# Sparse attention heads of a hybrid encoder block: negated logits, scaling by ScalarE, operands of two heads in one step, and some query copies by GpSimd's queue

## The chip, the cores and the metric

The kernel runs on one core of one Trainium2 chip. The metric is the device time of one execution in microseconds, as a median over runs; 439.57 us before the change. A profile of one execution gives the rows that this document quotes. In them PE is TensorE (its matmuls), PEld its weight loads, DVE is VectorE, ACT is ScalarE, POOL is GpSimd and SP is SyncE, which issues most DMAs. A name with a q (SPq, POOLq) is the engine's instruction queue. L389 is line 389 of the kernel's source.

## The reference

One pre-norm layer on x of 512 x 1024 in float32, with two token mixers that share one input projection. Cut to what matters:

```python
h = rmsnorm(x, norm_g)
(q_lat, c_kv, k_rope, z_a, q_b, k_b, v_b, z_b, q_idx, k_idx, w_idx, gate_a, gate_b) = split(h @ w_in)
# A: latent attention, 8 heads of 64 + 32 rotary, chunk-causal (chunks of 64)
y_a = mla_attention(...) * silu(z_a)
# B: sparse attention, 8 heads of 64; an indexer of 8 heads of 32 scores the keys
s     = einsum('qhd,kd->qhk', q_idx, k_idx) * 32 ** -0.5
score = einsum('qhk,qh->qk', relu(s), w_idx * 8 ** -0.5)      # inadmissible keys: -inf
idx   = top_k(score, 128)                                     # 128 keys for each query
logits = q_b . k_b[idx] * 64 ** -0.5 + rel_bias[t5_bucket(idx - pos)]
y_b   = softmax(logits) @ v_b[idx] * silu(z_b)
merged = sigmoid(gate_a) * (y_a @ w_o_a) + sigmoid(gate_b) * (y_b @ w_o_b)
out = rmsnorm(x + merged @ w_out, final_g)
```

## The kernel before

Every float32 product is made of products of rounded parts: an operand x is split into a high part (ScalarE rounds it) and a low part x - high (VectorE or GpSimd subtracts), and a product is high*high + high*low + low*high, three matmuls (`mm3`, recorded at L389).

The sparse heads do not gather keys. For each of the four tiles of 128 queries, the indexer's scores (`scores`) become a mask (`topk`: 16 rounds of the eight largest, for three tiles), which is 0 for chosen keys and -1e30 for the others. `dsa_base` loads the relative bias of a head and adds the mask (`s_p<-s_bias,mask`), so that a head starts from a tile `p` with bias plus mask. `dsa_head` then makes the logits of one tile on TensorE, and its `soft` adds them to `p` and takes the row maximum in one VectorE instruction (L1248), negates the maximum (L336, called from `soft`), applies the exponential on ScalarE with the row sum as a side result (L300), takes the reciprocal (L1142) and scales the row (`normalise`, by VectorE at L347 or GpSimd at L350). `attend` transposes the probabilities on TensorE (L406), splits them again and multiplies them with the values.

`dsa_jobs(j)` prepares the operands of heads 2j and 2j+1, which come out of one projection as rows 0 to 63 and 64 to 127 of one PSUM bank. A query operand is one tile with the high part in the head's own 64 rows and the low part in the other 64; a key operand is a tile with the high part in both halves and one with the low part in both halves. So two matmuls of 128 rows make the four products. `take_q` does this head by head with ScalarE and VectorE, each of which writes across to the other half; `take_k` makes the head's own half with these engines and the other half by a copy (`s_op<-s_op`, 128 KB, by SP's queue).

For the indexer, `take_qi` makes the query operand of each of eight heads out of three pieces of 32 rows, by 24 copies (`s_qs<-s_th`, 64 KB). The pieces whose number is below `QPOOL` go by GpSimd's queue, the others by SP's; `QPOOL` is 0.

The order of all work on every engine is fixed when the program is built. `Flow` is a planner: every piece of work is a generator that yields steps with one or more engines that may do them and an expected duration each, and waits for buffers (`Get`) or conditions (`Until`). At each turn the planner places the step that can start first, with a priority of 0.01 us per unit to break near ties; where a step may go to several engines, it takes the one that would end first, with a handicap or bonus for GpSimd (`pbias`) and for ScalarE (`ABIAS`, 0). On the chip each engine goes through its instructions in that order and waits for what they need. A DMA issued by SP is charged 0.05 us of SP, 0.65 us of the issuing hardware when both ends are tiles, 0.65 us more, its bytes at 360 GB/s, and 2.2 us till it has landed (1.0 us where it comes from or goes to HBM). A DMA by GpSimd is charged 1.03 us of that engine.

Weights come through four raw buffers (`fetcher`), are split into at most eight slots (`splitter`), and are used in the order of a list, `QUEUE` (`multiplier`): gates (ga, gb), silu paths (za, zb), head projections (ma, sb), values (va, vb). The four `sb` entries stand among gates and silu paths. The last products of the branches (`branch_out`, `s_ys,s_w`) come after all of them, first branch A's eight, then branch B's, and then those with `w_out`. TensorE fills with this list whenever no head's step can start sooner. Two lanes run the sparse heads, even and odd ones.

Of the kernel before, what the change touches and what calls it, by code (L numbers as in the profile page):

```python
# [13 lines left out]
AF = mybir.ActivationFunctionType  # L14
# [4 lines left out]
P = 128  # L19
# [60 lines left out]
class Step:  # L80


    moves = 0.0
    pair = False
    pbias = None
# [45 lines left out]
class Flow:  # L131
# [46 lines left out]
    def run(self, stop=None):  # L178
        while self.threads:
            if stop and stop():  # L180
                return
            moved = False
            for t in sorted(self.threads, key=lambda t: t.prio):
                if isinstance(t.req, Get):
                    b = t.req.pool.give(t.req)
                    if b is not None:
                        self.advance(t, b)
                        moved = True
                elif isinstance(t.req, Until) and t.req.cond():
                    self.advance(t, None)  # L190
                    moved = True
            if moved:
                continue
            best = None
            for t in self.threads:
                if isinstance(t.req, Step):
                    for i, (eng, dur, emit) in enumerate(t.req.options):
                        s = self.start(t.req, eng)
                        key = (s + BIAS * t.prio, t.prio)
                        if len(t.req.options) > 1:  # L200
                            fin = s + dur + {"POOL": self.pbias if t.req.pbias is None else t.req.pbias, "ACT": ABIAS}.get(eng, 0.0)
# [32 lines left out]

RAW_LAG = {"DVE": 0.125, "POOL": 0.1, "ACT": 0.1}
BIAS = 0.01
ABIAS = 0.0
TC_ARGS = {}


# [1 line left out]
def tile_block(ctx: ExitStack, tc: tile.TileContext, a: dict, out: bass.AP, bias_dram: bass.AP):  # L242
# [61 lines left out]
    def act(dst, src, func=AF.Copy, scale=None, bias=None, accum=None):  # L304
        step = Step([act_opt(dst, src, func, scale, bias, accum)], bufs(dst, accum), bufs(src, scale, bias))
        step.count = 2 if accum is not None else 1
        return step
# [886 lines left out]

    def dsa_jobs(j):
        def take_q(ps):
            yield Until(lambda: ("a", NH - 1, 0) in operands)
            for b in range(2):
                own, oth = slice(64 * b, 64 * b + 64), slice(64 - 64 * b, 128 - 64 * b)
                q = yield Get(QHI)  # L1200
                yield act(q[own, :], ps[own, :], AF.Copy, scale=HD ** -0.5)
                yield stt(q[oth, :], ps[own, :], HD ** -0.5, q[own, :].f, ALU.mult, ALU.subtract)
                operands["b", 2 * j + b, 0] = q
            put(ps)

        def take_k(ps):
            for b in range(2):
                own, oth = slice(64 * b, 64 * b + 64), slice(64 - 64 * b, 128 - 64 * b)
                kh = yield slot("op")
                kl = yield slot("op")  # L1210
# [12 lines left out]
    def dsa_base(h):  # L1223

        yield is_done("bias", *(("mask", i) for i in range(1, NT)))
        yield Until(lambda: h < 2 or ("b", h - 2) in done)
        bias = yield slot("bias")
        yield dma(bias.all.f, bass.AP(bias_dram.tensor, h * NREL + 1, [[1, P], [1, S]]))
        slots, probs = yield from prob_tiles("p", 6)
        for i in range(NT):  # L1230
            n = P * (i + 1)
            yield tt(probs[i], backward(bias.all.f[:, :n]), mask[i].all, ALU.add, BOTH)
        put(bias)
        bases[h] = (slots, probs)

    def dsa_head(h):
# [7 lines left out]
        def soft(i, ps):  # L1244
            n = P * (i + 1)
            mx = yield Get(SMALL)
            p = probs[i]
            step = Step([("DVE", 0.1 + 0.00104 * n, lambda: nc.vector.tensor_tensor_reduce(  # L1248
                p.ap, ps.tile[:, :n], p.ap, op0=ALU.add, op1=ALU.max, scale=1.0, scalar=FILL,
                accum_out=mx.tile[:, 0:1]))], [mx, p.buf], [ps])  # L1250
            step.count = 2
            yield step
            put(ps)
            yield ts(mx[:, 1:2], mx[:, 0:1], -1.0, None, ALU.mult)
            yield act(p, p, AF.Exp, bias=mx[:, 1:2], scale=1.0, accum=mx[:, 2:3])
            yield from normalise(p, mx)
            put(mx)
            ready.add(i)

# [366 lines left out]
PSQ = 0.0  # L1626
PSET = 0.0
NORM = ('DVE', 'POOL')
NWARM = 7
XAT = 1  # L1630
QPOOL = 0
PHCAP = 4
WCAP = 8
TCAP = 5
# [89 lines left out]
```

## Time and profile before

| | before |
|---|---|
| median of 3 runs | 439.57 us (439.42 to 441.98) |
| the profiled execution | 439.49 us |
| its span, first to last instruction | 437.7 us |
| TensorE busy | 426.2 us, 2219 matmuls |
| TensorE weight loads busy | 364.7 us |
| VectorE busy | 345.1 us, 810 instructions |
| ScalarE busy | 244.6 us, 546 instructions |
| GpSimd busy | 125.3 us, 150 instructions |
| mean granted TensorE clock | 0.998 |

The execution lasts 1.8 us longer than its span. Matmuls are pipelined, so that a busy TensorE need not be at its peak; DMA-issuing instructions are not counted as busy. In a row of a group, the number after the bar is the group's busy time in us, then the mean duration of one in ns, and after the next bar the idle time of the engine just before them and what ended it.

### The profile page before, as it was taken

To read this page: it belongs to the slowest core of one execution; us is meant where nothing else is said; L and a number is where in the kernel's file an instruction comes from. 1 tells how busy PE (TensorE), PEld (TensorE's weight loads), DVE (VectorE), ACT (ScalarE), POOL (GpSimd) and SP (SyncE) were. 2 spreads that over 40 slices of the span, in tenths; PEclk is the share of its full clock that TensorE was granted. 3 is DMA by queue.
4 is the path that set the end of the run, shared out by engine and by line. 5 is a ranking of instruction groups with operands and counts; after the bars stand their busy time and mean duration, and the time that the engine had idled before them with its cause. 6 is when DMAs were issued, how large, how long until landed. Compare 5 with 4: busy or idle time off the path is not lost.

```text
span 437.7 us, 6862 instructions
## 1 busy us (share of the span) xinstructions
PE 426.2 (97%) x2219; PEld 364.7 (83%) x2219; DVE 345.1 (79%) x810; ACT 244.6 (56%) x546; POOL 125.3 (29%) x150
## 2 busy tenths in 40 slices
PE   8999999999999999999999999999999999999994
PEld 5899878888887888878899888998888888888883
DVE  5599589999999999794343977835776686999995
ACT  6976877557472757364333654734565553345633
POOL 2256966544555634000003120050000011001452
PEclk9999999999999999999999999999999999999999
DMA  8973441725337361414541216234116445538405
GB/s 260 393 251 92 111 146 55 204 82 138 98 84 209 79 185 33 120 43 144 145 148 45 73 73 144 82 112 133 60 50 216 168 152 185 179 111 288 145 1 192
DMA packets 26500, 59.45 MB, mean 136 GB/s; under 512 B 4072, under 2 KB 4600, under 8 KB 26464
## 3 DMA queue, kind: packets, MB, share of 16 engines
q1 hardware_dynamic: 25744, 58.05, 43.2%
q0 software_dynamic: 576, 0.83, 0.7%
q8 instruction: 17, 0.28, 0.3%
q14 instruction: 19, 0.16, 0.1%
q10 hardware_dynamic: 144, 0.13, 0.1%
HBM read 48.39 MB, written 2.12 MB: 115 GB/s over the span
## 4 chain that ended last, share of the span: by engine, by line
PE 73%; DVE 13%; DMA 4%; ACT 4%; issue 2%; POOL 1%; SPq 1%; POOLq 0%; DVEq 0%; ACTq 0%
PE ps L389 67%; PE ps L406 4%; DVE mask L787 3%; DVE sm L786 3%; DMA s_op<-s_op 2%; DVE sm L1163 1%; DMA raw<-w_kvl 1%; DMA s_op<-kpel 1%; ACT junk L300 1%; PE ps L764 1%; SPq L416 1%; DVE s_ph L317 1%; PE ps L1182 1%; DVE qhi L328 1%; DVE s_op L328 1%
## 5 line engine op out<-in xcount | busy, mean ns | idle before, releaser
L389 PE MATMUL ps<-s_h,s_w 128*128 128x512 f32 x768 | 189.4, 394 | 0.0
L389 PEld LDWEIGHTS ps<-s_h,s_w 128*128 128x128 f32 x768 | 140.9, 188 | 26.7 <-issue 0.2
L319 POOL TENSOR_TENSOR s_w<-raw,s_w 128x512 fp32r<-128x512 f32 (+2 forms) x38 | 45.1, 1197 | 99.0 <-DMA raw<-w_out 64.3
L291 ACT CAST s_w<-raw 128x512 fp32r<-128x512 f32 (+3 forms) x114 | 64.3, 591 | 4.2 <-PE ps L389 2.1
L317 DVE TENSOR_TENSOR s_w<-raw,s_w 128x512 fp32r<-128x512 f32 (+2 forms) x76 | 49.2, 670 | 12.2 <-ACT s_w L291 11.8
L319 POOL TENSOR_TENSOR s_p<-s_bias,mask 128x128 f32<-128x128 f32 (+3 forms) x19 | 14.4, 785 | 102.9 <-DMA s_bias<-bias_scratch 90.3
L389 PE MATMUL ps<-s_ys,s_w 128*128 128x512 f32 x192 | 43.7, 389 | 0.0
L389 PEld LDWEIGHTS ps<-s_ys,s_w 128*128 128x128 f32 x192 | 36.0, 188 | 7.5
L389 PE MATMUL ps<-s_wo,s_mg 128*128 128x512 f32 (+1 forms) x156 | 33.0, 373 | 0.0
L389 PE MATMUL ps<-s_w,s_xg 128*128 128x328 f32 (+1 forms) x192 | 32.4, 324 | 0.0
L389 PEld LDWEIGHTS ps<-s_w,s_xg 128*128 128x128 f32 x192 | 31.5, 188 | 0.8 <-DVE s_w L317 0.2
L389 PEld LDWEIGHTS ps<-s_wo,s_mg 128*128 128x128 f32 x156 | 27.6, 188 | 5.2
L787 DVE MATCH_REPLACE8 mask<-sm,mask 128x256 f32<-128x256 f32 (+2 forms) x48 | 25.9, 541 | 0.0
L786 DVE MAX8 sm<-mask 128x8 f32<-128x256 f32 (+2 forms) x48 | 25.6, 549 | 0.3
L300 ACT ACTIVATE s_p<-ps,sm 128x128 f32<-128x128 f32 (+3 forms) x32 | 16.8, 527 | 15.2 <-DVE sm L1163 13.4
L389 PE MATMUL ps<-s_w,s_h 128*128 128x256 f32 x192 | 23.8, 284 | 0.0
L389 PEld LDWEIGHTS ps<-s_w,s_h 128*128 128x128 f32 x192 | 23.4, 192 | 0.2
L300 ACT ACTIVATE s_p<-s_p,sm 128x128 f32<-128x128 f32 (+3 forms) x32 | 17.8, 558 | 9.9 <-DVE sm L336 9.8
L406 PE MATMUL ps<-ident,s_p 128*128 128x128 f32 x160 | 22.9, 273 | 0.0
L300 ACT ACTIVATE s_sig<-ps 128x512 f32<-128x512 f32 x16 | 9.6, 597 | 22.7 <-PE ps L389 22.5
L350 POOL TENSOR_SCALAR s_p<-s_p,sm 128x128 f32<-128x128 f32 (+3 forms) x31 | 16.1, 527 | 19.0 <-DVE sm L1142 18.8
L389 PE MATMUL ps<-s_lat,s_w 128*128 128x512 f32 x78 | 21.4, 398 | 0.0
(164 smaller groups left out, 723.5 us busy)
## 6 DMA issues: line engine op xcount, KB each, us to landing
raw<-w_out SPq DMA_DIRECT2D x18, 512.0 KB, 4.2
raw<-w_ga SPq DMA_DIRECT2D x8, 512.0 KB, 4.3
raw<-w_gb SPq DMA_DIRECT2D x8, 512.0 KB, 3.6
raw<-w_o SPq DMA_DIRECT2D x16, 256.0 KB, 3.8
s_op<-s_op SPq DMA_DIRECT2D x28, 128.0 KB, 2.3
s_x<-xT SPq DMA_DIRECT2D x8, 256.0 KB, 5.4
s_xn<-x SPq DMA_DIRECT2D x8, 256.0 KB, 5.4
raw<-w_za SPq DMA_DIRECT2D x4, 512.0 KB, 4.2
```

Of the source, the lines that this page charges most:

```text
L291: nc.scalar.copy(dst.ap, src.ap)
L300: nc.scalar.activation(dst.ap, src.ap, func, **kw)
L317: opts.append(("DVE", 0.07 + 0.00104 * x.n, lambda: nc.vector.tensor_tensor(dst.ap, x.ap, y.ap, op=op)))
L319: opts.append(("POOL", 0.15 + 0.0021 * x.n, lambda: nc.gpsimd.tensor_tensor(dst.ap, x.ap, y.ap, op=op)))
L328: lambda: nc.vector.scalar_tensor_tensor(dst.ap, x.ap, sc(s), y.ap, op0=op0, op1=op1))],
L350: lambda: nc.gpsimd.tensor_scalar(dst.ap, x.ap, s.ap, 1.0, ALU.mult, ALU.mult)))
L389: nc.tensor.matmul(ps.ap, l.ap, r.ap, start=start and i == 0, stop=stop and i == len(pairs) - 1, skip_group_check=more)
L406: nc.tensor.transpose(d.ap, s.ap, ident.tile)
L416: return Step([("SP", n / 360000.0, lambda: nc.sync.dma_start(d, s))], bufs(dst), bufs(src))
L764: yield pe(0.005 + n / 2400, [ps.all], [qs[h].all, ks[0].all], lambda: nc.tensor.matmul(ps.tile[:, :n], qs[h].tile[:96, TOK[i]], ks[0].til ...
L786: yield Step([("DVE", t, lambda: nc.vector.max(m8.tile, work.tile))], [m8], [work])
L787: yield Step([("DVE", t, lambda: nc.vector.match_replace(work.tile, m8.tile, work.tile, MARK))], [work], [m8])
```

## The change

Four things.

In `soft` of the sparse heads the VectorE instruction computes -(logits + p) and takes the row minimum, which is the negated maximum. The separate negation goes, and the exponential is taken with scale -1.

The scaling of the sparse heads' rows may go to VectorE or ScalarE instead of VectorE or GpSimd, and the planner counts ScalarE as ending 0.5 us earlier than it would (`NORM_BIAS`). The heads of branch A keep VectorE or GpSimd.

`take_q` and `take_k` split both heads' rows at once, with one ScalarE and one VectorE instruction of 128 rows, and bring the halves to their places by copies on SP's queue: three for the queries of a pair, six for the keys. A copy that overwrites rows waits until the copies that read them are done.

`QPOOL` becomes 1: 8 of the indexer's 24 copies are issued by GpSimd. Besides, the planner counts the load of a head's bias as landing 1.5 us later (`late`).

```diff
@@ Flow.run
-                            fin = s + dur + {"POOL": ..., "ACT": ABIAS}.get(eng, 0.0)
+                            fin = s + dur + {"POOL": ..., "ACT": t.req.abias}.get(eng, 0.0)
...
-                end = self.dma + (2.2 if step.ins and step.outs else 1.0)
+                end = self.dma + (2.2 if step.ins and step.outs else 1.0) + step.late
@@ normalise
-    def normalise(p, mx):
+    def normalise(p, mx, engs=None):
         yield Step([("DVE", 0.07, lambda: nc.vector.reciprocal(mx.tile[:, 3:4], mx.tile[:, 2:3]))], [mx], [mx])
-        yield scale_by(p, p, mx[:, 3:4], NORM)
+        step = scale_by(p, p, mx[:, 3:4], engs or NORM)
+        step.abias = NORM_BIAS if engs else 0.0
+        yield step
@@ dsa_jobs
         def take_q(ps):
             yield Until(lambda: ("a", NH - 1, 0) in operands)
-            for b in range(2):
-                own, oth = slice(64 * b, 64 * b + 64), slice(64 - 64 * b, 128 - 64 * b)
-                q = yield Get(QHI)
-                yield act(q[own, :], ps[own, :], AF.Copy, scale=HD ** -0.5)
-                yield stt(q[oth, :], ps[own, :], HD ** -0.5, q[own, :].f, ALU.mult, ALU.subtract)
-                operands["b", 2 * j + b, 0] = q
+            q = yield Get(QHI)
+            q2 = yield Get(QHI)
+            lo = yield slot("op")
+            yield from split_scaled(q.all, lo.all, ps.all, HD ** -0.5)
             put(ps)
+            first, second = slice(0, 64), slice(64, 128)
+            yield dma(q2[second, :].f, q[second, :].f)
+            yield dma(q2[first, :].f, lo[second, :].f)
+            yield dma(q[second, :].f, lo[first, :].f)
+            put(lo)
+            operands["b", 2 * j, 0] = q
+            operands["b", 2 * j + 1, 0] = q2
         def take_k(ps):
-            for b in range(2):
-                ...
-                yield act(kh[own, :], ps[own, :])
-                yield lo_part(kl[own, :], ps[own, :], kh[own, :])
-                yield dma(kh[oth, :].f, kh[own, :].f)
-                yield dma(kl[oth, :].f, kl[own, :].f)
-                operands["b", 2 * j + b, 1] = (kh, kl)
-            put(ps)
+            ...
+            yield act(hi.all, ps.all)
+            yield lo_part(lo.all, ps.all, hi.all)
+            put(ps)
+            for part in (hi, lo):
+                k = yield slot("op")
+                for rows in (first, second):
+                    yield dma(k[rows, :].f, part[first, :].f)
+                yield dma(part[first, :].f, part[second, :].f)
+                pairs.append(k)
+            operands["b", 2 * j, 1] = tuple(pairs)
+            operands["b", 2 * j + 1, 1] = (hi, lo)
@@ dsa_base
+        step.late = 1.5
@@ dsa_head, soft
-                p.ap, ps.tile[:, :n], p.ap, op0=ALU.add, op1=ALU.max, scale=1.0, scalar=FILL,
-                accum_out=mx.tile[:, 0:1]))], [mx, p.buf], [ps])
+                p.ap, ps.tile[:, :n], p.ap, op0=ALU.add, op1=ALU.min, scale=-1.0, scalar=-FILL,
+                accum_out=mx.tile[:, 1:2]))], [mx, p.buf], [ps])
...
-            yield ts(mx[:, 1:2], mx[:, 0:1], -1.0, None, ALU.mult)
-            yield act(p, p, AF.Exp, bias=mx[:, 1:2], scale=1.0, accum=mx[:, 2:3])
-            yield from normalise(p, mx)
+            yield act(p, p, AF.Exp, bias=mx[:, 1:2], scale=-1.0, accum=mx[:, 2:3])
+            yield from normalise(p, mx, NORM_B)
@@ constants
+NORM_B = ('DVE', 'ACT')
+NORM_BIAS = -0.5
-QPOOL = 0
+QPOOL = 1
```

More of the change, by code (lines that the diff above doesn't have):

```diff
@@ L80 @@
 class Step:
+    abias = 0.0
+    late = 0.0
     moves = 0.0
@@ L200, in run @@
                         if len(t.req.options) > 1:
-                            fin = s + dur + {"POOL": self.pbias if t.req.pbias is None else t.req.pbias, "ACT": ABIAS}.get(eng, 0.0)
+                            fin = s + dur + {"POOL": self.pbias if t.req.pbias is None else t.req.pbias, "ACT": t.req.abias}.get(eng, 0.0)
                             cand = (fin, s, eng, dur, emit, key)
@@ L236 @@
 BIAS = 0.01
-ABIAS = 0.0
 TC_ARGS = {}
@@ L1197, in take_q @@
             yield Until(lambda: ("a", NH - 1, 0) in operands)
[L1198 to L1216 removed]
+            q = yield Get(QHI)
+            q2 = yield Get(QHI)
+            lo = yield slot("op")
+            yield from split_scaled(q.all, lo.all, ps.all, HD ** -0.5)
+            put(ps)
+            first, second = slice(0, 64), slice(64, 128)
[5 more added lines that the diff above has]
+            operands["b", 2 * j + 1, 0] = q2
+        def take_k(ps):
+            first, second = slice(0, 64), slice(64, 128)
+            pairs = []
+            hi = yield slot("op")
+            lo = yield slot("op")
+            yield act(hi.all, ps.all)
+            yield lo_part(lo.all, ps.all, hi.all)
+            put(ps)
+            for part in (hi, lo):
[6 more added lines that the diff above has]
+            operands["b", 2 * j + 1, 1] = (hi, lo)
         proj("w_kb", j, take_k, 8)
@@ L1227, in dsa_base @@
         bias = yield slot("bias")
-        yield dma(bias.all.f, bass.AP(bias_dram.tensor, h * NREL + 1, [[1, P], [1, S]]))
+        step = dma(bias.all.f, bass.AP(bias_dram.tensor, h * NREL + 1, [[1, P], [1, S]]))
+        step.late = 1.5
+        yield step
         slots, probs = yield from prob_tiles("p", 6)
```

## The prediction

> **What bounds the kernel now.** I read the profile's page first, then the table of stretches, then TensorE's own waits.
>
> ```profile
> span 437.7 us, 6862 instructions
> PE 426.2 (97%) x2219; PEld 364.7 (83%) x2219; DVE 345.1 (79%) x810; ACT 244.6 (56%) x546; POOL 125.3 (29%) x150
> PE 73%; DVE 13%; DMA 4%; ACT 4%; issue 2%; POOL 1%; SPq 1%; POOLq 0%; DVEq 0%; ACTq 0%
> ```
>
> TensorE is busy for 426.2 of 437.7 us and holds 73% of the chain that ended last. VectorE, at 79%, holds 13%. A share averages over stages, so I look at the stretch in which the sparse heads run (185 to 330 us), at one without heads (200 to 236), at one late in the kernel (371 to 424), and at the early stretch of the indexer (39 to 56).
>
> ```profile
> 185.00:330.00 145.00, 143.97 (x798) 125.23 (x797) 93.39 (x266) 74.78 (x169) 14.34 (x18) 1.00 0.33 97
> 200.00:236.00 36.00, 36.00 (x206) 31.78 (x205) 13.04 (x21) 12.24 (x22) 3.35 (x4) 1.00 0.42 125
> 371.00:424.00 53.00, 53.00 (x247) 44.34 (x246) 52.49 (x97) 25.23 (x51) 12.67 (x5) 1.00 0.45 149
> 39.00:48.00 9.00, 9.00 (x54) 9.00 (x53) 5.99 (x9) 6.02 (x14) 8.97 (x8) 1.00 0.35 83
> 48.00:56.00 8.00, 7.47 (x42) 6.02 (x41) 5.61 (x10) 5.68 (x14) 7.72 (x11) 1.00 0.44 101
> ```
>
> The columns are the stretch, its length, then busy time (and instructions) of TensorE, its weight loads, VectorE, ScalarE, GpSimd, and the granted clock. Among the sparse heads TensorE lacks 145.00 - 143.97 = 1.03 us of being full, at clock 1.00, while VectorE has 51.6 us to spare. The change removes work of VectorE exactly there. VectorE is full only at 371 to 424, which the change doesn't touch, and there TensorE is full as well. So the removed VectorE work cannot itself be worth its length. It is worth the TensorE waits that it ends. These are few:
>
> ```profile
> PE ps L389 <- DVE qhi L328: 0.9, 2, 0.5
> PE ps L406 <- POOL s_latraw L350: 0.5, 2, 0.2
> PE ps L1182 <- DMA s_op<-kpel: 0.3, 1, 0.3
> PE ps L1181 <- DMA s_op<-kpel: 0.2, 1, 0.2
> L389 PEld LDWEIGHTS ps<-s_op,qhi 128*128 128x128 f32 x64 | 10.3, 188 | 2.9 <-DVE qhi L328 1.3 <-DMA s_op<-s_op 0.3
> L406 PEld LDWEIGHTS ps<-ident,s_latraw 128*128 128x128 f32 (+1 forms) x24 | 3.0, 135 | 1.7 <-POOL s_latraw L350 1.3
> ```
>
> The first four rows count idle time of the array, whose matmuls drain into a wait. The last two count the idle time of weight loading before the same matmuls, which is nearer to what the wait costs. In all: 1.3 us for the sparse queries (qhi), 1.3 us for the latent scaling (L350), 0.5 us for rotary keys that come by DMA (kpel).
>
> **Removed and moved, sparse heads.** The row for what feeds the first scores of a pair shows why TensorE waits:
>
> ```profile
> 185.13 0.59 ACT L300 ACTIVATE qhi<-ps 64x512 fp32r<-64x512 f32 x1 [2.13 <-PE ps L389]
> 185.75 0.68 DVE L328 SCALAR_TENSOR_TENSOR qhi<-ps,qhi 64x512 fp32r<-64x512 f32 x1 [1.20 <-ACT qhi L300]
> 186.47 0.59 ACT L300 ACTIVATE qhi<-ps 64x512 fp32r<-64x512 f32 x1 [0.75 <-DVE qhi L328]
> 187.10 0.69 DVE L328 SCALAR_TENSOR_TENSOR qhi<-ps,qhi 64x512 fp32r<-64x512 f32 x1 [0.66 <-ACT qhi L300]
> 187.85 1.56 PE L389 MATMUL ps<-s_op,qhi 128*128 128x256 f32 x8 [0.47 <-DVE qhi L328]
> ```
>
> The four steps run in series for 187.79 - 185.13 = 2.66 us, though the second pair does not need the first. After the change there is one ACT and one DVE step over 128 rows; a row of the same engine lasts by its columns, so I take 0.59 + 0.69 = 1.3 us. Then come three copies by SP's queue. The per-instruction prices:
>
> ```profile
> L336 DVE TENSOR_SCALAR sm<-sm 128x1 f32<-128x1 f32 x32 | 4.1, 143 | 0.1
> L347 DVE TENSOR_SCALAR s_p<-s_p,sm 128x128 f32<-128x128 f32 (+3 forms) x32 | 12.2, 393 | 0.1
> L328 DVE SCALAR_TENSOR_TENSOR qhi<-ps,qhi 64x512 fp32r<-64x512 f32 x8 | 5.5, 688 | 9.4 <-ACT qhi L300 9.4
> L317 DVE TENSOR_TENSOR s_op<-ps,s_op 64x512 fp32r<-64x512 f32 x8 | 5.5, 688 | 8.2 <-ACT s_op L291 8.1
> L300 ACT ACTIVATE s_p<-s_p,sm 128x128 f32<-128x128 f32 (+3 forms) x32 | 17.8, 558 | 9.9 <-DVE sm L336 9.8
> ```
>
> VectorE loses the 32 negations (4.1 us), up to 32 scalings (12.2 us), and half of the two splits (2.75 + 2.75 us): 21.8 us, nearly all inside 185 to 330, where its 93.4 us become some 72. ScalarE takes the scalings. No scaling by ScalarE in a head is in this trace; the nearest row is its exponential over the same four widths, 558 ns, so 32 x 0.558 = 17.9 us, and it loses half of 8 x 0.59 twice (4.7 us). Its 74.8 us become 88 of 145. Both engines are covered by TensorE there. If the cover were gone, a head would gain 0.14 us per tile from the missing negation and lose 0.56 - 0.39 = 0.17 by the slower scaling: nothing either way. The negated reduction (L1248) and the exponential with scale -1 keep their instructions and shapes; a negative factor could cost something only by another instruction, for which no row speaks, and 32 of them are covered too. I take 0 for all this, and -1.3 us for the wait for qhi, if the copies are in time.
>
> **Added: copies and a wait on SP's queue.** For each of four pairs the keys take 6 copies instead of 4 and the queries 3 instead of none, so 20 more.
>
> ```profile
> s_op<-s_op SPq DMA_DIRECT2D x28, 128.0 KB, 2.3
> 132.42 4.22 DMA s_op<-s_op
> 264.87 5.39 DMA s_op<-s_op
> 180.42 2.75 SPq L416 DMA_DIRECT2D s_op<-s_op  x4
> 172.68 0.33 SPq L416 DMA_DIRECT2D raw<-w_kb  x1
> 211.46 0.58 ACT L291 CAST s_op<-ps 64x512 fp32r<-64x512 f32 x1 [3.82 <-PE ps L389]
> 348.96 23.28 PE L389 MATMUL ps<-s_ys,s_w 128*128 128x512 f32 x102
> 329.86 0.68 DVE L317 TENSOR_TENSOR s_y<-s_y,s_z 128x512 f32<-128x512 f32 x1
> ```
>
> Issuing costs SP 2.75 / 4 = 0.69 us each, 14 us over 140. A copy lands after 2.3 us, or after 4.22 and 5.39 beside a weight load. The third copy overwrites rows that the first two read, so SP must wait for those: the key's chain is three landings (two copies, the third with the low part's pair, the last), 7 to 14 us, the query's is two, 5 to 10 us. Scores start perhaps 4 to 8 us later than now. What stands behind that wait on SP are weight loads, and they run far ahead: the key weights issued at 172.68 are used up when their result is read at 211.46, 38.8 us later. TensorE meanwhile has gates and projections. The last pair's gated result is ready at 329.86 and is read only in the second half of the products that begin at 348.96, so a head that is 8 us late costs nothing.
>
> What could cost is only an error of the plan: TensorE's order is fixed at build, so scores placed too early hold everything behind them. The plan gives a copy 0.65 + 0.65 + 0.36 + 2.2 = 3.9 us (Flow.run and dma), above the usual 2.3 and below 5.39. Copies already feed scores in the trace, with TensorE waits of 0.3 us (s_op) and 0.5 us (kpel) over the twelve projections that they serve. Bounds for the four new places: 0, and 4 x (5.39 - 3.9) x 3 links = 18 us. Nearest are the measured waits, so I take 0.3 us.
>
> **Moved: a third of the indexer's queries.**
>
> ```profile
> 39.21 16.70 SPq L416 DMA_DIRECT2D s_qs<-s_th  x24
> 44.85 0.63 POOL L420 DMA_DIRECT2D s_raw<-onehot  x1
> s_qs<-s_th SPq DMA_DIRECT2D x24, 64.0 KB, 2.0
> s_raw<-onehot POOLq DMA_DIRECT2D x2, 80.0 KB, 3.4
> ```
>
> SP loses 8 x 16.70 / 24 = 5.6 us, so queries and the weight loads after them come up to 5.6 us earlier. GpSimd gets 8 x 0.63 = 5.0 us in a stretch in which it is busy 8.97 of 9.00 and 7.72 of 8.00 us. So its compute must move: VectorE has 3.0 + 2.4 us free there and ScalarE 3.0 + 2.3, about as much. Late behind it would be the latent scaling, which TensorE already waits for (1.3 us). Scaling may go to any of the three engines; a full GpSimd pushes it to VectorE or ScalarE. Bounds: -1.3 us if that wait goes, +5.0 us if the issues fall on the path. I take -0.5 us, since the planner charges GpSimd 1.03 us for each issue (pool_dma), more than the 0.63 seen, and so moves work away in time.
>
> The Trainium skill speaks against this part: "DMA: Bandwidth & Descriptors", section "SWDGE vs HWDGE vs iDMA", says that GpSimd writes descriptors by software into SBUF rings and can be locked out by VectorE's two-port modes, which SP's path never is. The landing of 3.4 against 2.0 us agrees in sign; by it alone the first queries would land 1.4 us later, and since scores have other TensorE work beside them the sum would stay.
>
> The bias load's planned lateness (1.5 us) adds no instruction; eight loads are only placed otherwise.
>
> **The sum.** The profiled execution took 439.49 us, 1.8 more than its span, and the median of the runs is 439.57. So 439.5 - 1.3 (qhi) + 0.3 (new copies) - 0.5 (latent scaling) = 438.0 us.
>
> **Rivals.** First, late copies: the chain of three landings is later than planned beside weight loads. For it speak the 4.22 and 5.39 us; against it, that most copies take 2.3, and that a plan of 3.9 for each leaves slack. With one slow link in each pair, TensorE is held 4 x 1.5 = 6.0 us, and 439.5 - 1.3 + 6.0 - 0.5 = 443.7; with a little more, 445. It decides from 0.45 us lateness for each pair on, where the gain of 1.8 is eaten. Chance 0.17.
>
> Second, GpSimd as the early bound: 5.0 us of issues delay splits and latent scaling where it has no room. TensorE loses up to 5.0 - 0.5: 439.5 - 1.3 + 0.3 + 4.5 = 443.0. Against it speaks the room on the other two engines. Chance 0.08.
>
> Third, all waits named go, since everything is placed anew: 439.5 - 1.3 - 1.3 - 0.5 - 0.3 = 436.1; with small bubbles among the early heads, 435. Chance 0.15.
>
> Fourth, the change doesn't do what it says: the planner leaves scalings on VectorE. TensorE covers them either way; 438 to 439.5. Chance 0.05. The forecast keeps 0.55.
>
> **How the numbers follow.** About 1% (4.4 us) is what a measurement of this kernel can tell from no change; the limits are 435.2 and 443.9. Faster by more takes nearly every TensorE wait in the trace: half of the third rival's far side, 0.08. Slower by more takes the worse half of the first two rivals (0.12) and what a new order may break elsewhere (0.05): 0.17. Within 1%: 0.75. The range runs from 435.4, where the waits are gone, to 443.5, where one slow link in each pair counts.
>
> **What would show it.** Right: the wait of L389 for qhi gone from TensorE's list, no wait for copies over 0.5 us, VectorE about 20 us less busy and ScalarE about 13 more, at a TensorE busy time of 426 us. Wrong: TensorE rows waiting for copies into s_op or qhi, or idle time between 39 and 60 us that names GpSimd or a query copy. A time under 435 would mean that TensorE's 426 us are not the floor I take them for.

## The result and the profile after

The changed kernel takes 438.79 us (median of 20 runs, 438.40 to 440.29), the kernel before takes 439.97 us (20 runs beside it). The ratio is 0.9977 with a 95% interval of 0.9966 to 0.9987: a gain of 0.6 to 1.5 us, which is less than the 1% at which the prediction set its limits. The forecast was a gain of 1.5 us. Direction and size agree, but two of the terms do not: the one for `qhi` was too small, the one for `QPOOL` is about nothing in place of -0.5, and the two errors cancel.

The head of the page of the changed kernel, and its chain of work that ended last:

```profile
span 437.0 us, 6841 instructions
...
PE 424.6 (97%) x2219; PEld 364.0 (83%) x2219; DVE 334.9 (77%) x752; ACT 248.1 (57%) x564; POOL 117.8 (27%) x150
...
PE 77%; DVE 13%; issue 3%; ACT 2%; POOL 1%; DMA 1%; SPq 1%; POOLq 0%; DVEq 0%
```

TensorE has the same 2219 matmuls and bounds the kernel still. VectorE lost 10.2 us of work (345.1 before), GpSimd 7.5; ScalarE gained only 3.5. The table of stretches, with the columns that the prediction names:

```profile
39.00:48.00 9.00, 9.00 (x54) 9.00 (x53) 6.42 (x6) 4.32 (x10) 7.63 (x9) 1.00 0.24 55
48.00:56.00 8.00, 7.02 (x40) 5.75 (x39) 5.00 (x9) 7.93 (x20) 7.55 (x10) 1.00 0.43 133
185.00:330.00 145.00, 145.00 (x803) 126.34 (x802) 80.38 (x206) 77.09 (x181) 10.72 (x14) 1.00 0.41 119
```

Among the sparse heads TensorE is now full, 145.00 of 145.00 us (143.97 before), and VectorE has 13.0 us less to do (93.39 before). From 48 to 56 it is the other way: TensorE is busy 7.02 us where it was 7.47. TensorE's list of waits (us in total, times, longest) shows what replaced the old ones:

```profile
PE ps L484 <- DVE junk L444: 1.5, 1, 1.5
PE ps L765 <- DVE mask L329: 1.4, 1, 1.4
PE ps L765 <- DVE s_qs L318: 1.0, 1, 1.0
PE ps L407 <- POOL rstd L368: 0.9, 1, 0.9
PE ps L390 <- ACT s_xg L301: 0.4, 1, 0.4
```

The waits for qhi, for the latent scaling and for kpel are gone. The first, fourth and fifth rows belong to the first 20 us and stand in nearly every kernel here with changing lengths. New are the two waits of the indexer's scores (L765), 2.4 us together. The groups that answer to those of before:

```profile
L301 ACT ACTIVATE s_p<-s_p,sm 128x128 f32<-128x128 f32 (+3 forms) x55 | 28.1, 547 | 10.6 <-DVE sm L1264 9.9 <-DVE sm L1143 0.7
...
L1264 DVE CUSTOM_DVE_ANT_0 s_p<-ps,s_p 128x128 f32<-128x128 f32 (+3 forms) x32 | 14.8, 483 | 7.1 <-PE ps L390 7.1
...
L390 PEld LDWEIGHTS ps<-s_op,qhi 128*128 128x128 f32 x64 | 10.2, 188 | 1.3 <-DMA s_op<-s_op 0.2
...
L348 DVE TENSOR_SCALAR s_p<-s_p,sm 128x256 f32<-128x256 f32 (+3 forms) x9 | 3.5, 402 | 0.2
...
L407 PEld LDWEIGHTS ps<-ident,s_latraw 128*128 128x128 f32 (+1 forms) x24 | 2.8, 135 | 0.9 <-DVE mask L337 0.5
```

55 - 32 = 23 of the 32 scalings went to ScalarE and 9 stayed on VectorE. Weight loading sat idle before the sparse scores for 1.3 us in place of 2.9, and for 0.2 us of it a copy was late.

**Where the time is.** A list of waits leaves out delays that don't show as idle, so I use one more number, worked out from the trace: for every matmul the time from its start to the next one's start, less the median of that time over all matmuls of its shape, summed over a stretch. What is left is the time by which TensorE fell behind its own pace. All kernels have the same matmuls, and the span less this sum is 427.3 to 428.2 us in all of them; so the sum carries the differences to within 0.9 us. For single executions that is as much as the change gains, and the table serves to place a loss, not to measure the gain.

| lost by TensorE, us | 0-20 | 20-80 | 80-180 | 180-340 | sum |
|---|---|---|---|---|---|
| before | 2.1 | 2.1 | 3.2 | 2.9 | 10.2 |
| after | 1.9 | 4.5 | 1.3 | 1.0 | 8.8 |
| e1: QPOOL = 1 alone | 2.2 | 4.6 | 1.4 | 2.6 | 10.8 |
| e2: pairs alone | 2.0 | 2.0 | 3.2 | 1.9 | 9.1 |
| e3: softmax alone | 2.1 | 2.1 | 3.2 | 3.8 | 11.1 |
| e4: after, QPOOL = 0 | 2.4 | 2.1 | 3.2 | 0.9 | 8.6 |
| e5: e4, 8 copies by GpSimd | 2.4 | 5.1 | 3.2 | 0.9 | 11.6 |
| e6: after, all copies by SP | 2.2 | 2.2 | 1.1 | 1.3 | 6.8 |
| e11: e1, all copies by SP | 1.8 | 2.3 | 1.2 | 2.6 | 7.8 |

After less before: +2.4 from 20 to 80 us (indexer), -1.9 from 80 to 180 (heads of branch A and the top-k), -1.9 from 180 to 340 (sparse heads). That is -1.5 in all. The span of this one execution fell by 0.7 only, since span less sum is 428.2 against 427.4; the medians, over 20 runs each, differ by 1.2.

### The profile page after: what moved, and what is told of

Same layout as the page of the kernel before. It is cut to its first block, busy times and chain, and to the rows that moved or that the text cites. A ratio compares the mean times of both kernels' runs of the same rounds, so it can differ in the third digit from the quotient of the medians.

```text
span 437.0 us, 6841 instructions
## 1 busy us (share of the span) xinstructions
PE 424.6 (97%) x2219; PEld 364.0 (83%) x2219; DVE 334.9 (77%) x752; ACT 248.1 (57%) x564; POOL 117.8 (27%) x150
## 4 chain that ended last, share of the span: by engine, by line
PE 77%; DVE 13%; issue 3%; ACT 2%; POOL 1%; DMA 1%; SPq 1%; POOLq 0%; DVEq 0%
PE ps L390 69%; PE ps L407 4%; DVE s_wo L318 2%; DVE s_mg L318 2%; DVE s_sig L318 1%; PE ps L1184 1%; PE ps L1185 1%; PE ps L1186 1%; DMA raw<-w_kvl 1%; DVE s_wsum L318 1%; DVE s_sig L329 1%; DVE s_xr L329 1%; ACT junk L301 1%; SPq L417 1%; DVE s_rg L329 1%
## 5 line engine op out<-in xcount | busy, mean ns | idle before, releaser
L320 POOL TENSOR_TENSOR s_w<-raw,s_w 128x512 fp32r<-128x512 f32 (+2 forms) x36 | 44.0, 1228 | 53.8 <-ACT s_w L292 28.9
L320 POOL TENSOR_TENSOR s_p<-s_bias,mask 128x128 f32<-128x128 f32 (+3 forms) x13 | 9.4, 752 | 107.2 <-DMA s_bias<-bias_scratch 102.2
L301 ACT ACTIVATE s_p<-s_p,sm 128x128 f32<-128x128 f32 (+3 forms) x55 | 28.1, 547 | 10.6 <-DVE sm L1264 9.9
L292 ACT COPY s_tmp<-ps 64x512 f32<-64x512 f32 (+1 forms) x18 | 10.1, 562 | 19.6 <-PE ps L390 19.5
```

Of the source, the lines that this page charges most:

```text
L292: nc.scalar.copy(dst.ap, src.ap)
L301: nc.scalar.activation(dst.ap, src.ap, func, **kw)
L320: opts.append(("POOL", 0.15 + 0.0021 * x.n, lambda: nc.gpsimd.tensor_tensor(dst.ap, x.ap, y.ap, op=op)))
```

## The experiments

My theory was that the gain is the end of the qhi waits and comes from the operands of two heads (pairs); the rivals were that it comes from VectorE's relief (softmax), or that the copies or GpSimd's issues cost what the pairs gain. Each time stands beside runs of the kernel before on the same chip (439.5 to 439.7 us).

| run | us | ratio to before | 95% interval |
|---|---|---|---|
| e1_pool_queue_alone | 440.92 | 1.0027 | 1.0016 to 1.0038 |
| e2_pairs_alone | 438.80 | 0.9983 | 0.9972 to 0.9995 |
| e3_softmax_alone | 440.47 | 1.0021 | 1.0012 to 1.0031 |
| e4_after_sp_queue | 438.34 | 0.9967 | 0.9955 to 0.9979 |
| e5_sp_plan_pool_issue | 441.41 | 1.0040 | 1.0027 to 1.0053 |
| e6_pool_plan_sp_issue | 436.08 | 0.9921 | 0.9908 to 0.9933 |
| e7_copies_twice | 483.74 | 1.1007 | 1.0980 to 1.1034 |
| e8_pairs_negated | 438.19 | 0.9965 | 0.9953 to 0.9977 |
| e9_pairs_scalar_scaling | 437.56 | 0.9962 | 0.9949 to 0.9975 |
| e10_latent_off_gpsimd | 443.84 | 1.0101 | 1.0079 to 1.0123 |
| e11_before_pool_plan_sp_issue | 437.70 | 0.9959 | 0.9947 to 0.9971 |
| e12_six_idle_copies | 441.31 | 1.0051 | 1.0032 to 1.0070 |

### Each part by itself: e1 to e4

e1, the kernel before with one constant changed:

```diff
-QPOOL = 0
+QPOOL = 1
```

> The kernel before with QPOOL = 1 alone. Operand theory (the change gains where the sparse pairs no longer hold TensorE for qhi, and the query copies by GpSimd's queue lose part of it): the early waits of the changed kernel come with this part, so TensorE waits 1 to 2.5 us for the indexer's scores between 50 and 80 us, the latent-scaling wait goes, the qhi waits stay, and the time is 0 to 1.5 us above before. Relief theory (less VectorE work brings the gain): no gain here, time equal to before within 0.5 us. Placement theory (every new order brings its own waits, whatever the edit): early waits of any sign, between -2 and +2 us.

Measured: 1.2 us slower. TensorE's waits:

```profile
PE ps L764 <- DVE mask L328: 1.4, 1, 1.4
PE ps L389 <- DVE qhi L328: 1.1, 2, 0.6
PE ps L764 <- DVE s_qs L317: 0.9, 1, 0.9
```

Both score waits come with this part; the qhi waits stay.

e2, the kernel before with the new `take_q` and `take_k`:

```diff
-            for b in range(2):
-                ...
+            yield from split_scaled(q.all, lo.all, ps.all, HD ** -0.5)
+            yield dma(q2[second, :].f, q[second, :].f)
+            ...
```

> The kernel before with only the operands of two heads made at once (take_q and take_k). Operand theory: the wait of the sparse scores for qhi is gone, no wait for copies above 0.3 us in its place, early waits as before, and the time is 1 to 2 us below before (ratio 0.995 to 0.998), at least as fast as the full change. Relief theory: only a quarter of the relieved VectorE time is in this part (5.5 of 21.8 us), so at most 0.5 us. Placement theory: between -2 and +2 us without a pattern.

Measured: 0.2 to 1.2 us faster, where 1 to 2 had been expected. No wait for qhi is left. Two of the rows of its list that are new:

```profile
PE ps L389 <- DVE s_ph L317: 0.5, 1, 0.5
...
PE ps L389 <- DVE s_last L317: 0.4, 1, 0.4
```

The second wait is at 328 us, at the end of the last pair: from 320 to 330 us TensorE loses 1.2 us where it lost 0.2. So the heads' later start does cost something when nothing else is changed.

e3, the kernel before with negated logits and scaling by VectorE or ScalarE:

```diff
-    op0=ALU.add, op1=ALU.max, scale=1.0, scalar=FILL, accum_out=mx.tile[:, 0:1]
+    op0=ALU.add, op1=ALU.min, scale=-1.0, scalar=-FILL, accum_out=mx.tile[:, 1:2]
-            yield ts(mx[:, 1:2], mx[:, 0:1], -1.0, None, ALU.mult)
-            yield from normalise(p, mx)
+            yield from normalise(p, mx, NORM_B)
```

> The kernel before with only the negated logits and the scaling of the sparse heads by VectorE or ScalarE. Operand theory: TensorE covers VectorE there, so the qhi waits stay (1.3 us by the weight loads) and the time equals before within 0.7 us, though VectorE has some 16 us less to do. Relief theory: three quarters of the relieved VectorE time is here, so 0.8 to 1.2 us below before. Placement theory: between -2 and +2 us.

Measured: 0.5 to 1.4 us slower (at most 0.7 had been expected), though VectorE is busy for 335.8 us (345.1 before). Two rows of TensorE's waits:

```profile
PE ps L390 <- DVE qhi L329: 0.9, 2, 0.5
PE ps L390 <- DMA s_op<-s_op: 0.9, 2, 0.6
```

The qhi waits are untouched, and at 269 us the scores of a pair now come before their key copies have landed. VectorE's relief is not the source of the gain.

e4, the change with QPOOL = 0:

```diff
-QPOOL = 1
+QPOOL = 0
```

> The changed kernel with QPOOL = 0, so that all the indexer's copies are issued by SP again. Operand theory: the waits for the scores at 53 and 75 us of the changed kernel are gone, the wait for latent scaling may come back (1.3 us), the qhi waits stay away, and the time is 0 to 1.5 us below the changed kernel, 437.3 to 438.8. Relief theory: no difference from the changed kernel. Placement theory: between -2 and +2 us against the changed kernel.

Measured: 0.9 to 2.0 us faster than before. No score wait, no qhi wait; the latent wait is back (0.6 us in three places in TensorE's list). Against the changed kernel it is 0.4 us faster, which the intervals do not tell apart: the part QPOOL = 1, a loss when made alone (e1), is worth about nothing inside the change, though its two halves are large.

### The new order and the new queue: e5, e6, e11

QPOOL does two things: GpSimd issues eight copies, and the planner, who counts on that, writes another order for all engines. These three kernels part the two. e5 has the order of e4, but the eight first pieces are in fact issued by GpSimd, at the places where the plan had SP:

```diff
+    step = dma(d, s)
+    if c == 0:
+        step.options = [("SP", ..., lambda: nc.gpsimd.dma_start(d.ap, s.ap))]
+    yield step
```

> The changed kernel planned with all 24 query copies on SP (QPOOL = 0), but the 8 copies of the first piece are in fact issued by GpSimd at the places that the plan gave them. It has the planner's order of e4_after_sp_queue and the queue of the changed kernel. Order theory (the copies strung out by a planner that charges GpSimd 1.03 us each make the early score waits): no waits for scores at 54 and 75 us, time that of e4_after_sp_queue within 0.6 us, 437.7 to 439. Queue theory (copies by GpSimd are slow in themselves, or take the port from VectorE): score waits or late latent scaling come back, 0.8 to 2 us above e4_after_sp_queue.

Measured: 441.41 us, (1.0040 - 0.9967) x 439.6 = 3.2 us more than e4. TensorE's first waits, then GpSimd's rows from the timeline of e5 and of e4:

```profile
PE ps L390 <- POOL s_w L320: 1.9, 1, 1.9
...
PE ps L407 <- POOL s_latraw L351: 1.3, 4, 0.6
```

```profile
47.49 1.48 POOL L730 DMA_DIRECT2D s_qs<-s_th  x3
48.99 2.53 POOL L320 TENSOR_TENSOR s_h<-s_tmp,s_h 128x512 fp32r<-128x512 f32 x2
51.46 3.75 POOL L320 TENSOR_TENSOR s_w<-raw,s_w 128x512 fp32r<-128x512 f32 x3
```

```profile
48.36 3.81 POOL L320 TENSOR_TENSOR s_w<-raw,s_w 128x512 fp32r<-128x512 f32 x3
```

Each issue holds GpSimd for about half a microsecond (1.48 / 3). Its splits of weights start at 51.46 instead of 48.36, and TensorE waits for them, and for the latent scaling behind them. This is the second rival of the prediction, as it was described, and it costs more than the 0.8 to 2 us that the queue theory gave.

e6 is the opposite: the order of the changed kernel, but SP issues the copies where the plan had GpSimd.

```diff
-    yield from pool_dma(d, s)
+    step = next(pool_dma(d, s))
+    step.options = [("POOL", ..., lambda: nc.sync.dma_start(d.ap, s.ap))]
+    yield step
```

> The changed kernel with its own plan (QPOOL = 1), but the 8 copies are in fact issued by SP at the places that the plan gave them. Order theory: the waits for scores near 54 us (1.0) and 75 us (1.4) stay, time that of the changed kernel within 0.6 us. Queue theory: the waits shrink to under 0.5 us and the time falls to that of e4_after_sp_queue, about 438.3.

Measured: 436.08 us, 0.9921 of before (0.9908 to 0.9933). It beats both kernels, and it is some 2 us below what either theory gave: the queue theory had the loss by the issues, and neither had a gain by the order. The one TensorE wait that its list has behind the first 20 us:

```profile
PE ps L768 <- DVE s_qs L318: 0.4, 1, 0.4
```

e11 does the same to e1, so without pairs and softmax:

```diff
-QPOOL = 0
+QPOOL = 1
...
+    step.options = [("POOL", ..., lambda: nc.sync.dma_start(d.ap, s.ap))]
```

> The kernel before with the plan of QPOOL = 1, but all copies in fact issued by SP. Beside e1_pool_queue_alone (440.92) it gives the price of GpSimd's issue without the other parts. Queue theory: 2 to 3 us below e1_pool_queue_alone, so 438 to 439, with the qhi waits still there (1.3 us) and the waits for scores under 0.6 us. Order theory: 440.3 to 441.3, as e1_pool_queue_alone.

Measured: 437.70 us, 1.8 us faster than before (438 to 439 had been expected), with the qhi waits in place:

```profile
PE ps L389 <- DVE qhi L328: 1.0, 2, 0.5
```

So the issues by GpSimd cost 3.2 us (e5 less e4), 3.0 (e1 less e11) and 2.5 (after less e6), from the differences of the ratios; and the order planned for them is worth 2.0 us (e6 against e4) and 1.8 (e11 against before). The table puts the cost into 20 to 80 us (2.3 to 3.0) and the gain into 80 to 180 (1.8 to 2.1, in every kernel with that plan and in none without). Why the other order is better there I did not settle: VectorE is busy for some 98 of these 100 us in both, and small waits of branch A's heads for GpSimd, VectorE and copies go. By the table's number, sorted by the matmul that starts late, the matmuls of these heads' scores, transposes and products with the values are 2.6 us late in all before and 0.6 after.

### Softmax beside the pairs: e8, e9

e8 is e2 with the negated logits; e9 is e4 with the maximum and its negation in two instructions again, so e2 with scaling by ScalarE. Besides, e4 and e9 count the load of a head's bias as landing later (`late`), which e2 and e8 do not; no run tries that by itself.

```diff
-            yield ts(mx[:, 1:2], mx[:, 0:1], -1.0, None, ALU.mult)
-            yield act(p, p, AF.Exp, bias=mx[:, 1:2], scale=1.0, accum=mx[:, 2:3])
+            yield act(p, p, AF.Exp, bias=mx[:, 1:2], scale=-1.0, accum=mx[:, 2:3])
```

(This is e8's edit behind the negated reduction; e9 has it the other way round.)

> The kernel before with the operands of two heads at once and the negated logits, but scaling by VectorE or GpSimd as before. Operand theory with a tail (with later heads the softmax of the last pair holds TensorE: 0.2 us for the scaled rows and 0.4 us for their split in e2_pairs_alone near 325 us): the negation alone saves 0.14 us for each tile, so these waits shrink little and the time is within 0.5 us of e2_pairs_alone, 438.3 to 439.3. Relief theory: a quarter of the relieved VectorE time of the softmax part is here, so about 0.3 us below e2_pairs_alone; the rest is ScalarE's scaling.

> The changed kernel with QPOOL = 0 and with the maximum and its negation as two VectorE instructions, as before: operands of two heads at once and scaling by VectorE or ScalarE. With e2_pairs_alone (438.80), e8_pairs_negated (438.19) and e4_after_sp_queue (438.34) it completes a square. Operand theory: once the pairs' operands no longer hold TensorE, neither negation nor scaling is worth more than the small softmax waits of the last pair (0.6 us in e2_pairs_alone): 437.7 to 439.0. Relief theory: scaling is three quarters of the softmax's relieved time, so it is the faster half, 437.9 or less.

Measured: 438.19 and 437.56 us. From 180 to 340 us TensorE loses 1.9 us with pairs alone (e2), 1.2 with the negation, 0.8 with the scaling, 0.9 with both (e4). The waits at the end of the last pair, which e2 shows, go with either. The ratios, 0.9983, 0.9965, 0.9962 and 0.9967, have intervals that overlap: one softmax part is worth 0.8 or 0.9 us beside the pairs by the middle values, which is not told apart from nothing, and the second adds nothing. Both medians lie 0.1 us under the range that the operand theory had given, and e9's in the range of the relief theory (437.9 or less); these runs do not decide between the two.

### The copies: e7, e12

e7 issues six of a pair's nine copies twice. The plan is that of e4.

```diff
+    step.options = [(eng, t, lambda: (emit(), emit()))]
```

> The changed kernel with QPOOL = 0, in which each copy of take_q and take_k that reads another head's rows before they are overwritten (2 for the queries, 4 for the keys of a pair) is issued twice, without the plan knowing: 24 copies and some 16 us more of SP, and every third copy waits longer. If the copies have slack (the forecast's reading: planned at 3.9 us, landing at 2.3 to 3, and heads that may be 8 us late), TensorE waits for s_op or qhi grow to at most 0.5 us for each pair: 0 to 2 us above e4_after_sp_queue. If they are at the edge (the rival of late copies), each of the four pairs is late by two more issues and a longer landing in three links, 2 to 4 us: 6 us or more above it.

Measured: 483.74 us. The second copy writes what the first wrote and so waits for its landing (SP waits 40.8 us for `s_op` copies, where it waits 9.5 us in the changed kernel); the chain grew by whole landings and not by issues, so that this run does not give the price I was after. What it gives is the scale of the first rival:

```profile
PE ps L390 <- DMA qhi<-s_op: 26.7, 3, 9.9
PE ps L390 <- DMA s_op<-s_op: 7.0, 3, 2.6
```

Three of the four pairs hold TensorE for some 11 us each; the second does not, because its heads wait for the ones before them in their lanes. During and behind each of these waits the granted clock is about 0.50 for 10 to 14 us (199 to 213, 298 to 308 and 349 to 363 us), which is part of the 45 us over e4 too.

e12 puts extra copies of 64 rows by 64 columns, into tiles that nothing reads, behind six of the nine copies of each pair; the plan doesn't know of them. No copy repeats another here, but one that overwrites rows waits for the extra copies that read them as well as for the others: in the third pair it starts at 267.19, just behind the landing of the second extra copy (267.11; the copy that this one stands behind landed at 266.94). So the chain grew by issues and a little more.

```diff
+    step.options = [(eng, t, lambda: (emit(), nc.sync.dma_start(d, s)))]
```

> The changed kernel with QPOOL = 0 and six more small copies for each pair, into tiles that nothing reads, right behind the first copies of the queries and keys; the plan does not know them. Unlike in e7_copies_twice no copy waits for one that it repeats, so that the chain of a pair grows by issue time alone, 4 x 0.6 us for the keys and up to 1.2 us for the queries. Hidden, as the forecast costed the added copies: at most 0.5 us for each pair, 0 to 1.5 us above e4_after_sp_queue. At the edge, as the gaps between the last landing and the first score in the traces read (0 to 1.2 us for three pairs, 17 us for the second): the three pairs without slack are late by 1 to 3 us each, 3 to 8 us above it.

Measured: 441.31 us, (1.0051 - 0.9967) x 439.6 = 3.7 us more than e4 by the ratios.

```profile
PE ps L390 <- DMA s_op<-s_op: 2.6, 3, 1.5
```

Again three pairs of four. A delay of six issues (at half a microsecond or so, 3 us a pair) holds TensorE for about 1 us a pair. So from the last copy to the first score there is little room. In the changed kernel itself, the first pair's last copy for the keys and a weight load of its first scores (timelines of SP and of weight loads):

```profile
189.34 0.46 SPq L417 DMA_DIRECT2D s_op<-s_op  x1
```

```profile
195.20 0.19 PEld L390 LDWEIGHTS ps<-s_op,qhi 128*128 128x128 f32 x1 [0.20 <-DMA s_op<-s_op]
```

This copy was issued 0.7 us after a load of weights and landed at 195.16 by its semaphore, 5.8 us later; the median of its group is 3.0. The weight load waited 0.2 us for it.

### Off GpSimd: e10

If the latent wait in e4 is GpSimd's queue, the scaling may go to VectorE or ScalarE alone:

```diff
-    scale_by(raw..., rl[:, t : t + 1], ("DVE", "POOL", "ACT"))
+    scale_by(raw..., rl[:, t : t + 1], ("DVE", "ACT"))
```

> The changed kernel with QPOOL = 0, and the scaling of the latents allowed to VectorE and ScalarE only. If GpSimd's 0.56 us for each tile is what TensorE waits for at 54 us (1.4 us by the weight loads in e4_after_sp_queue), this wait goes below 0.5 us and the time is 0.8 to 1.4 us below e4_after_sp_queue, 437.0 to 437.6. If any new order brings its own waits (placement theory), it is anywhere from 436.5 to 440.

Measured: 443.84 us, slower than e4 by (1.0101 - 0.9967) x 439.6 = 5.9 us where a gain was expected, and outside the range of the placement theory (436.5 to 440) as well. TensorE's waits, the scaling's durations (min/median/max in ns), and two stretches:

```profile
PE ps L407 <- DVE s_latraw L348: 3.0, 2, 2.3
```

```profile
L348 DVE TENSOR_SCALAR s_latraw<-s_latraw,sm x3: 405/1200/1423, 55.0 to 56.7; 128x384 f32<-128x384 f32 x3
```

```profile
56.00:59.00 3.00, 1.46 (x6) 0.84 (x7) 2.93 (x6) 1.27 (x3) 1.19 (x2) 0.97 0.66 171
59.00:62.00 3.00, 3.00 (x11) 2.51 (x11) 2.44 (x4) 1.22 (x3) 1.27 (x1) 0.50 0.33 135
```

The scaling left GpSimd, but it still needs a factor that GpSimd makes behind its splits (it starts at 54.99; in e4 at 53.69). On VectorE two of three last 1.2 and 1.4 us: they end 0.2 us behind a GpSimd split that runs at the same time (54.94 to 56.20 and 56.66 to 57.65), and the one that falls between the splits takes 0.405. TensorE waits 3.0 us, and then runs at half its clock for some 3 us (granted 0.50 from 59 to 62, the third last number of the row; matmuls of 512 columns start every 427 ns instead of 227). From 20 to 80 us it loses 6.9 us against 2.1. An offload counts by what the work still waits for and by whom it meets there.

## Why the prediction was right, point by point

**TensorE is the bound, and VectorE's relief is worth nothing by itself.** Right. e3 takes 9.3 us from VectorE and is slower. The pairs end the qhi waits (e2, e4), which was the term of -1.3 us; from 180 to 340 us the changed kernel loses 1.9 us less than before. The term was too small: by the table's number the matmuls of the sparse scores start 2.0 us late in all before, 0.2 in e2 and after, and 3.0 in e3, so that the pairs end 1.8 us there, of which 1.3 showed as idle time of the weight loads.

**Copies: +0.3 us.** The size was right (0.2 us of weight loading waits for a copy), the reason given was too generous. The chain is late by 7 us, within the 4 to 8 that the prediction foresaw: the first scores start at 195.05, not 187.85. But "a head that is 8 us late costs nothing" failed in e2, where the last pair loses 1.0 us more at its end. In the full change the lighter softmax gives that back, which is the one thing that the relief is good for. And the copies land with 0, 14.5, 1.2 and 0.4 us to spare (from each pair's last landing to its first scores in the trace of the changed kernel; the 17 in the expectation of e12 is too much), not behind a broad cover: the late copies of the first rival are real, and e12 reaches them with half a microsecond or so for each issue. The groups of copies and SP's wait for them, after:

```profile
s_op<-s_op SPq DMA_DIRECT2D x36, 128.0 KB, 3.0
...
qhi<-s_op SPq DMA_DIRECT2D x8, 128.0 KB, 3.1
```

```profile
SPq L417 <- DMA s_op<-s_op: 9.5, 9, 2.3
```

The median went from 2.3 to 3.0 us, still under the 3.9 that the plan allows. Single copies took longer, the 5.8 us above and 4.9 and 4.6 us for the last two of the fourth pair, and there the plan held with 0.4 us left. SP waits 9.5 us for copies, and nothing behind it was late for TensorE: that step was right.

**Scalings and ScalarE.** I let all 32 go to ScalarE; 23 went. VectorE's stretch fell to 80.4 and not to 72: the nine scalings are 3.5 us of that, and the rest is mostly other work that the planner put there, four more splits of weights (43 for 39) and five more additions of the mask (12 for 7). ScalarE rose to 77.1, not to 88, though the scalings that it got add 12.2 us of durations: busy time counts once what overlaps, and of some work of the last heads the stretch holds less. The price, 0.558 us each, was right (547 ns over exponentials and scalings; 12.2 / 23 = 0.53), and the negated reduction costs what the old one did (483 against 484 ns). Since TensorE covers both, the error moved nothing.

**QPOOL: -0.5 us. This is the step that failed.** It was the sum of two large terms that the forecast did not have. The planner's charge of 1.03 us for an issue was said to protect, being more than the 0.63 seen. It does move work: GpSimd's 39 to 48 us fall from 8.97 to 7.63 busy, and the latent wait of 1.3 us goes, as taken (by the table's number, from 1.2 us to 0.3). But it does not make the issues harmless, and the copies go out late. SP's first and last ones and GpSimd's first and last ones after, and the last of the same eight in e6:

```profile
41.40 2.51 SPq L417 DMA_DIRECT2D s_qs<-s_th  x4
...
79.71 1.57 SPq L417 DMA_DIRECT2D s_qs<-s_th  x2
```

```profile
43.10 0.61 POOL L421 DMA_DIRECT2D s_qs<-s_th  x1
...
73.06 0.54 POOL L421 DMA_DIRECT2D s_qs<-s_th  x1
73.62 1.30 POOL L320 TENSOR_TENSOR s_tmp<-s_tmp,ropes 128x512 f32<-128x512 f32 x1
74.87 1.28 POOL L320 TENSOR_TENSOR s_w<-raw,s_w 128x512 fp32r<-128x512 f32 x1
```

```profile
71.50 0.52 SPq L730 DMA_DIRECT2D s_qs<-s_th  x1
```

"Queries and the weight loads after them come up to 5.6 us earlier" held for the first weight loads (at 48.68 and 52.28 us, before at 56.02 and 56.84) and was wrong for the queries: before, SP had issued all 24 by 55.91; now GpSimd's last goes at 73.06 and SP's last two from 79.71 on. This lateness lies in the new order and is not what costs: e6 has it too, with SP issuing, and is the fastest kernel. What costs is GpSimd's issuing. In the order of e4 it pushes GpSimd's splits and the scalings of the latents back (e5). In the new order it comes out at the indexer's scores, whose matmuls start 2.9 us late in all from 20 to 80 us by the table's number, against 0.7 in e6 and none before. The landing was not slower: the eight copies by GpSimd's queue land after 2.0 us in the median, SP's sixteen after 2.6. The slower landing by GpSimd (3.4 against 2.0), which the prediction read from another transfer, did not come up here.

The chance of 0.08 for the second rival was too low for its mechanism: eight issues by GpSimd cost 2.5 to 3.2 us in all three comparisons. The forecast came out right because the order that the planner writes with QPOOL = 1 ends about 2 us of delays at 80 to 180 us, a stretch for which its sum has no term (0.5 us of waits for kpel there stand in its third rival). That was luck: nothing in the prediction's mechanism gives it. What the change could have had is that order with SP's queue, e6: 2.5 us less than the changed kernel by the ratios.

**The claims on what would show it.** No copy wait over 0.5 us and no qhi wait: so it was. VectorE 20 us less and ScalarE 13 more: 10 and 3.5. The sign named for being wrong, idle time at 39 to 60 that names GpSimd or a query copy, did not come up by that name: the wait at 54.9 us (1.0 us) names VectorE, which writes the low part of the indexer's keys there (their tile is called s_qs too) behind a scaling that waits for a factor from GpSimd, and the larger one lies at 77.

## What to carry to other kernels

Where one engine is full, cost an edit by the waits of that engine that it ends, and not by the work it removes elsewhere. With a planned order, an edit to a queue has two effects, the queue and the order written for it; keep the order and swap the queue alone (and the reverse) before judging either, since here one cost 3 us and the other gained 2. And before adding transfers to a chain, read the time from the last landing to the first use: a plan can be right and still leave no room.

## What the hardware showed

One VectorE instruction tells how the issues hurt late. In the changed kernel it is the sum of two SBUF tiles, and TensorE's matmul at the end of its chain:

```profile
73.44 3.27 DVE L318 TENSOR_TENSOR s_tmp<-s_tmp,s_tmp 128x512 f32<-128x512 f32 x1
76.63 1.26 DVE L329 SCALAR_TENSOR_TENSOR mask<-ps,widx,mask 128x384 f32<-128x384 f32 x2
```

```profile
77.29 0.50 PE L765 MATMUL ps<-s_qs,s_qs 96*128 96x512 f32 x1 [1.37 <-DVE mask L329]
```

and in e6, with the same order but no issue on GpSimd, VectorE and then GpSimd:

```profile
73.08 1.48 DVE L318 TENSOR_TENSOR s_tmp<-s_tmp,s_tmp 128x512 f32<-128x512 f32 x1
```

```profile
72.71 1.30 POOL L320 TENSOR_TENSOR s_tmp<-s_tmp,ropes 128x512 f32<-128x512 f32 x1
73.96 1.76 POOL L320 TENSOR_TENSOR s_w<-raw,s_w 128x512 fp32r<-128x512 f32 x1
```

The same instruction takes 0.69 us at 79.29 in e6, when GpSimd is idle. Beside GpSimd it lasted until one of GpSimd's instructions had ended in e6 (73.08 + 1.48 = 74.56, that is 0.60 after 73.96), and until two had ended in the changed kernel (76.71 against 74.87 + 1.28 = 76.15). The Trainium skill, "SBUF — State Buffer", section "Who interferes with whom", says that a VectorE instruction with two SBUF inputs and a GpSimd instruction that reads SBUF exclude each other, and that whichever issues first has the shared port for the whole instruction. The blocking agrees with these rows; who wins does not follow from the recorded starts, since VectorE's 73.44 is earlier than GpSimd's 73.62. That the issue at 73.06 is what turned the order was not tried by itself.

The clock after the waits of e10 was the second surprise: 2.32 us of idle array and another 0.69 us came before a granted clock of 0.50 over 59 to 62 us. The Trainium skill, "TensorE: Matmul & The Clock Gate", Part 1, gives two states, full and half, and half after an idle window of about 3.4 us. The value agrees; the array was not idle for such a window here, it had run three matmuls in between. A wait can thus cost more than its length; the 1.9 us of e5 and the 1.4 us of the changed kernel were not followed by it (granted clock 1.00 from 52 to 58 and from 75 to 78 us).
